# A row maximum that skips NaN: two engines in place on 16-bit halves, 64 KB loads, groups of rows with their own store

## The chip, the cores and the metric

One core of a Trainium2 chip. All times are device microseconds (us) of one execution; a kernel's time is the median of its runs. The experiments were spread over three chips; the kernel before, run beside each, took 1297.36 to 1297.54 us on all three, so I subtract their times. ACT is ScalarE, DVE is VectorE, POOL is GpSimd, SP is the queue that issues the loads.

## The reference

```python
x = np.random.randn(32, 2048, 2048).astype(np.float32)   # 537 MB
x[np.random.rand(32, 2048, 2048) < 0.1] = np.nan
return np.nanmax(x, axis=-1).astype(np.float32)           # 65536 results
```

There are 65536 rows of 2048 numbers: 512 rows for each of the 128 partitions. Every byte is read once, so the loads alone set a floor.

## The kernel before

It reads the floats as integers. ACT turns each into a key, the square of its distance from a large constant, so that NaN gets a large key and the greatest float the smallest. DVE takes the minimum. A load brings 4 rows to each partition (4 MB in all).

```python
io = ctx.enter_context(tc.tile_pool(name="io", bufs=3))      # loads, 32 KB per partition each
keys = ctx.enter_context(tc.tile_pool(name="keys", bufs=2))  # keys, another 32 KB each
for m in range(M):                                           # 128 times
    xt = io.tile([P, C, D], i32)
    nc.sync.dma_start(out=xt, in_=x_ck[m])
    kt = keys.tile([P, C, D], f32)
    nc.scalar.activation(out=kt, in_=xt, func=Square, bias=bias_t, scale=SCALE)
    nc.vector.tensor_reduce(out=acc[:, m, :], in_=kt, axis=X, op=min)
# ... cut: a square root on ACT with two Newton steps on DVE for all 512 columns,
# ... 64 transposes of 32 x 32 to bring the results into the order of the output, one store
```

The activation writes to another buffer, so a load buffer is free again as soon as ACT has read it.

Of the kernel before, what the change touches and what calls it, by code (L numbers as in the profile page):

```python
# [1 line left out]

# [4 lines left out]


@with_exitstack  # L10
def kernel(
    ctx: ExitStack,
    tc: tile.TileContext,
    x: bass.AP,
    axis: bass.AP,
    out: bass.AP,
):
    nc = tc.nc
    P = nc.NUM_PARTITIONS
    f32 = mybir.dt.float32  # L20
    i32 = mybir.dt.int32

    nd = len(x.shape)
    assert axis in (-1, nd - 1), axis
    D = x.shape[-1]

    x_bits = x.bitcast(i32).flatten_outer_dims()
    R = x_bits.shape[0]
    C = 4
    assert R % (P * C) == 0  # L30
    M = R // (P * C)
    x_ck = x_bits.rearrange("(m p c) d -> m p c d", p=P, c=C)

    out_flat = out.flatten_outer_dims().rearrange("r c -> (r c)")
    out_pn = out_flat.rearrange("(q s) -> q s", q=P)

    CG = float(0x50000000)
    SCALE = 2.0**-31
    BIAS = -CG * SCALE

    io = ctx.enter_context(tc.tile_pool(name="io", bufs=3))
    keys = ctx.enter_context(tc.tile_pool(name="keys", bufs=2))
    sing = ctx.enter_context(tc.tile_pool(name="sing", bufs=1))

    bias_t = sing.tile([P, 1], f32)
    nc.vector.memset(bias_t, BIAS)  # L46
    acc = sing.tile([P, M, C], f32)

    for m in range(M):
        xt = io.tile([P, C, D], i32)  # L50
        nc.sync.dma_start(out=xt, in_=x_ck[m])  # L51
        kt = keys.tile([P, C, D], f32)
        nc.scalar.activation(  # L53
            out=kt,
            in_=xt,
            func=mybir.ActivationFunctionType.Square,
            bias=bias_t,
            scale=SCALE,
        )
        nc.vector.tensor_reduce(  # L60
            out=acc[:, m, :],
            in_=kt,
            axis=mybir.AxisListType.X,
            op=mybir.AluOpType.min,
        )

    NQ = M * C
    accf = acc.rearrange("p m c -> p (m c)")
    y = sing.tile([P, NQ], f32)
    nc.scalar.activation(y, accf, mybir.ActivationFunctionType.Sqrt)  # L70
    for it in range(2):
        r = sing.tile([P, NQ], f32, tag=f"nr{it}")
        nc.vector.reciprocal(r, y)  # L73
        t = sing.tile([P, NQ], f32, tag=f"nt{it}")
        nc.vector.tensor_mul(t, accf, r)  # L75
        s = sing.tile([P, NQ], f32, tag=f"ns{it}")
        nc.vector.tensor_add(s, t, y)  # L77
        y = sing.tile([P, NQ], f32, tag=f"ny{it}")
        nc.vector.tensor_scalar_mul(y, s, 0.5)  # L79
    gf = sing.tile([P, NQ], f32)  # L80
    nc.scalar.activation(  # L81
        gf,
        y,
        mybir.ActivationFunctionType.Copy,
        bias=CG,
        scale=-(2.0**31),
    )
    gb = sing.tile([P, NQ], i32)
    nc.vector.tensor_copy(out=gb, in_=gf)  # L89

    B = 32
    assert M % P == 0
    U = M // P
    fin = sing.tile([P, U, P, C], i32)
    g4 = gb.rearrange("p (q u c) -> p q u c", u=U, c=C)
    for u in range(U):
        for j in range(C):
            for bi in range(P // B):
                for bj in range(P // B):
                    nc.vector.transpose(  # L100
                        out=fin[bi * B : (bi + 1) * B, u, bj * B : (bj + 1) * B, j],
                        in_=g4[bj * B : (bj + 1) * B, bi * B : (bi + 1) * B, u, j],
                    )
    nc.sync.dma_start(
        out=out_pn, in_=fin.rearrange("q u p c -> q (u p c)").bitcast(f32)
    )


# [1 line left out]
_INS = ['x', 'axis']  # L110
_OUTS = [((32, 2048), 'float32')]
#: Inputs that are plain numbers.
_NUMBERS = {'axis': -1}


# [26 lines left out]
```

## Time and profile before

1297.49 us (3 runs, 1297.33 to 1297.58). The head of the page gives each engine's busy time:

```profile
span 1295.8 us, 761 instructions
DVE 1138.4 (88%) x202; ACT 915.4 (71%) x132; POOL 0.2 (0%) x4
...
q1 hardware_dynamic: 18576, 537.14, 96.4%
```

The windows view gives the main part without start and end (columns: stretch, its length, busy us of each engine with its instructions, clock, share of DMA engines busy, GB/s):

```profile
core 0: us, DVE busy (x) ACT busy (x) POOL busy (x), PEclk, DMA share, GB/s
100.00:1200.00 1100.00, 982.71 (x114) 805.41 (x114) 0.00 (x0) 1.00 1.00 432
```

The DMA engines are never idle there: this kernel is bound by its loads, at 432 GB/s. The groups of instructions give what the stages take (after the bar: busy us, mean ns of one; after the second bar: idle us before, and what ended it):

```profile
L60 DVE TENSOR_REDUCE acc<-kt 128x4 f32<-128x8192 f32 x128 | 1111.7, 8686 | 151.2 <-ACT kt L53 151.2
L53 ACT ACTIVATE kt<-xt,bias_t 128x8192 f32<-128x8192 int32 x128 | 911.6, 7122 | 329.1 <-DMA xt<-in_x_dram 329.1
```

And the waits of the load queue say who frees the buffers (us in total, times, longest):

```profile
SPq L51 <- ACT kt L53: 899.4, 125, 8.5
SPq L51 <- DMA xt<-in_x_dram: 277.6, 125, 11.0
```

The timeline of the end (start us, us, engine, operation):

```profile
1247.91 7.12 ACT L53 ACTIVATE kt<-xt,bias_t 128x8192 f32<-128x8192 int32 x1 [2.58 <-DMA xt<-in_x_dram]
...
1255.06 8.69 DVE L60 TENSOR_REDUCE acc<-kt 128x4 f32<-128x8192 f32 x1 [1.02 <-ACT kt L53]
1263.78 0.63 ACT L70 ACTIVATE y<-acc 128x512 f32<-128x512 f32 x1 [7.45 <-DVE acc L60]
...
1276.17 16.70 DVE L100 STREAM_TRANSPOSE fin<-gb 32x32 int32<-32x32 int32 x64
1292.89 0.35 SPq L104 DMA_DIRECT2D out_dram<-fin  x1
```

The last load landed at 1247.8; the remaining 48 us are a tail in which nothing is loaded.

### The profile page before, as it was taken

Reading aid. Unit: us, or ns where it says so; the run is one execution under the profiler, and the core shown is the slowest. Engines: PE = TensorE matmul, PEld = TensorE weight load, DVE = VectorE, ACT = ScalarE, POOL = GpSimd, SP = SyncE. Lnnn points to the kernel's source line nnn. Section 1 sums busy time; section 2 is a strip of 40 time slices with the busy share of each in tenths; the row PEclk is TensorE's granted clock in tenths of the full one; section 3 lists DMA queues with packets and bytes.
Section 4 is the critical chain, followed back from the end, with each engine's and each line's share of the span. In section 5 each row is a group of like instructions: output and inputs, shape, how many; then the busy total and the mean of one; then the engine's idle time right before and its main releaser. Section 6 shows DMA issues by size and latency. Waiting matters only on the chain.

```text
span 1295.8 us, 761 instructions
## 1 busy us (share of the span) xinstructions
DVE 1138.4 (88%) x202; ACT 915.4 (71%) x132; POOL 0.2 (0%) x4
## 2 busy tenths in 40 slices
DVE  3988988988988988998998998998898998998998
ACT  4776776776776777777777777777777777777760
POOL 0000000000000000000000000000000000000000
DMA  9999999999999999999999999999999999999940
GB/s 405 437 426 432 437 429 429 437 433 426 435 432 428 434 433 427 435 435 425 435 435 425 436 434 426 435 435 426 433 436 428 431 436 430 429 436 430 429 196 8
DMA packets 18582, 537.19 MB, mean 415 GB/s; under 512 B 2064, under 2 KB 2064, under 8 KB 2192
## 3 DMA queue, kind: packets, MB, share of 16 engines
q1 hardware_dynamic: 18576, 537.14, 96.4%
q14 instruction: 6, 0.05, 0.0%
HBM read 536.87 MB, written 0.26 MB: 415 GB/s over the span
## 4 chain that ended last, share of the span: by engine, by line
DMA 73%; ACT 24%; DVE 3%; issue 0%; ACTq 0%; SPq 0%; DVEq 0%
DMA xt<-in_x_dram 73%; ACT kt L53 24%; DVE fin L100 1%; DVE acc L60 1%; DVE r L73 1%; DVE t L75 0%; DVE s L77 0%; DVE y L79 0%; ACTq L53 0%; ACT y L70 0%; ACT gf L81 0%; DVE gb L89 0%; SPq L51 0%; DVEq L137 0%
## 5 line engine op out<-in xcount | busy, mean ns | idle before, releaser
L60 DVE TENSOR_REDUCE acc<-kt 128x4 f32<-128x8192 f32 x128 | 1111.7, 8686 | 151.2 <-ACT kt L53 151.2
L53 ACT ACTIVATE kt<-xt,bias_t 128x8192 f32<-128x8192 int32 x128 | 911.6, 7122 | 329.1 <-DMA xt<-in_x_dram 329.1
L100 DVE STREAM_TRANSPOSE fin<-gb 32x32 int32<-32x32 int32 x64 | 15.8, 248 | 0.9
L53 ACT ACT_TABLE_LOAD x1 | 1.3, 1283 | 13.1 <-DMA xt<-in_x_dram 13.1
L81 ACT ACTIVATE gf<-y 128x512 f32<-128x512 f32 x1 | 0.6, 629 | 10.6 <-DVE y L79 10.6
L73 DVE RECIPROCAL r<-y 128x512 f32<-128x512 f32 x2 | 6.7, 3353 | 0.7 <-ACT y L70 0.7
L70 ACT ACTIVATE y<-acc 128x512 f32<-128x512 f32 x1 | 0.6, 629 | 7.5 <-DVE acc L60 7.5
L75 DVE TENSOR_TENSOR t<-acc,r 128x512 f32<-128x512 f32 x2 | 1.4, 693 | 0.1
L77 DVE TENSOR_TENSOR s<-t,y 128x512 f32<-128x512 f32 x2 | 1.4, 691 | 0.1
L70 ACT ACT_TABLE_LOAD x1 | 1.3, 1283 | 0.0
L89 DVE CAST gb<-gf 128x512 int32<-128x512 f32 x1 | 0.4, 427 | 0.7 <-ACT gf L81 0.7
L79 DVE TENSOR_SCALAR y<-s 128x512 f32<-128x512 f32 x2 | 0.9, 426 | 0.1
L46 DVE MEMSET bias_t<- 128x1 f32 x1 | 0.1, 59 | 0.8 <-PEq L123 0.8
L123 POOL MEMSET const-bfloat16-1.0<- 128x1 bf16 x1 | 0.1, 102 | 0.0
L123 POOL MEMSET const-uint8-127<- 128x1 uint8 x1 | 0.1, 102 | 0.0
L123 POOL MEMSET const-float32-0.0<- 128x1 f32 x1 | 0.1, 99 | 0.2 <-issue 0.2
L123 POOL MEMSET const-float32-1.0<- 128x1 f32 x1 | 0.1, 99 | 0.0
## 6 DMA issues: line engine op xcount, KB each, us to landing
xt<-in_x_dram SPq DMA_DIRECT2D x128, 4096.0 KB, 21.9
out_dram<-fin SPq DMA_DIRECT2D x1, 256.0 KB, 2.0
```

Of the source, the lines that this page charges most:

```text
L46: nc.vector.memset(bias_t, BIAS)
L53: nc.scalar.activation(out=kt, in_=xt, func=mybir.ActivationFunctionType.Square, bias=bias_t, scale=SCALE,)
L60: nc.vector.tensor_reduce(out=acc[:, m, :], in_=kt, axis=mybir.AxisListType.X, op=mybir.AluOpType.min,)
L70: nc.scalar.activation(y, accf, mybir.ActivationFunctionType.Sqrt)
L73: nc.vector.reciprocal(r, y)
L75: nc.vector.tensor_mul(t, accf, r)
L77: nc.vector.tensor_add(s, t, y)
L79: nc.vector.tensor_scalar_mul(y, s, 0.5)
L81: nc.scalar.activation(gf, y, mybir.ActivationFunctionType.Copy, bias=CG, scale=-(2.0**31),)
L89: nc.vector.tensor_copy(out=gb, in_=gf)
L100: nc.vector.transpose(out=fin[bi * B : (bi + 1) * B, u, bj * B : (bj + 1) * B, j], in_=g4[bj * B : (bj + 1) * B, bi * B : (bi + 1) * B, u, j],
L123: nc = _bacc.Bacc("TRN2", target_bir_lowering=False, num_devices=1)
```

## The change

Its intent: larger loads (8 rows, 64 KB per partition), no separate key buffers, so that three such loads fit, and almost no tail. ACT and POOL rewrite the upper 16 bits of each float in place, so that every NaN becomes a number below all others; DVE takes a plain float maximum, which is already the result. Rows are dealt out in groups in which a partition's results lie next to each other in the output, so the transposes go; each group has its own small finish (`none`, `fin`) and store; the last loads become shorter and shorter.

```diff
+GROUPS = [(40, [8] * 5)] * 12 + [(24, [7, 6, 5, 4, 2]), (8, [2, 2, 1, 1, 1, 1])]
     io = ctx.enter_context(tc.tile_pool(name="io", bufs=3))
-    keys = ctx.enter_context(tc.tile_pool(name="keys", bufs=2))
+    res = ctx.enter_context(tc.tile_pool(name="res", bufs=3))
 ... (cut)
+    for s, cuts in GROUPS:
 ... (cut: xg and og, the group's part of the input and of the output; at counts its rows)
+        acc = res.tile([P, s], f32, tag="acc")
+        for c in cuts:
+            xt = io.tile([P, c * D], i32, tag="xt")
+            nc.sync.dma_start(out=xt, in_=xg[:, at : at + c]...)
+            nc.scalar.activation(out=xt.bitcast(u16)[:, 1::2], in_=xt.bitcast(i16)[:, 1::2],
+                func=Prelu, bias=top, scale=-1.0, alpha=...)
+            nc.gpsimd.tensor_scalar(out=xt.bitcast(i16)[:, 1::2], in0=xt.bitcast(u16)[:, 1::2],
+                scalar1=-1.0, scalar2=float(TOP), op0=mult, op1=add)
+            nc.vector.tensor_reduce(out=acc[:, at : at + c], in_=xt.bitcast(f32)..., op=max)
+        none = res.tile([P, s], i32, tag="none")
+        nc.vector.tensor_scalar(out=none, in0=acc, ..., op0=is_equal, op1=mult)
+        fin = res.tile([P, s], i32, tag="fin")
+        nc.vector.tensor_tensor(out=fin, in0=acc.bitcast(i32), in1=none, op=bitwise_or)
+        nc.scalar.dma_start(out=og, in_=fin)
-    (cut: the square root, Newton steps, transposes and the one store at the end)
```

More of the change, by code (lines that the diff above doesn't have):

```diff
@@ L7 @@
 from concourse._compat import with_exitstack
+GROUPS = [(40, [8] * 5)] * 12 + [
+    (24, [7, 6, 5, 4, 2]),
+    (8, [2, 2, 1, 1, 1, 1]),
+]
+TOP = 0x7F7F
+NAN = 0x7FC0
+LOW = -129
+EDGE = TOP + 0.25
+NONE = -255.0 * 2.0**120
 @with_exitstack
@@ L19 @@
     P = nc.NUM_PARTITIONS
-    f32 = mybir.dt.float32
-    i32 = mybir.dt.int32
+    f32, i32 = mybir.dt.float32, mybir.dt.int32
+    i16, u16 = mybir.dt.int16, mybir.dt.uint16
+    ALU = mybir.AluOpType
     nd = len(x.shape)
@@ L25 @@
     D = x.shape[-1]
-    x_bits = x.bitcast(i32).flatten_outer_dims()
-    R = x_bits.shape[0]
-    C = 4
-    assert R % (P * C) == 0
-    M = R // (P * C)
-    x_ck = x_bits.rearrange("(m p c) d -> m p c d", p=P, c=C)
-    out_flat = out.flatten_outer_dims().rearrange("r c -> (r c)")
-    out_pn = out_flat.rearrange("(q s) -> q s", q=P)
-    CG = float(0x50000000)
-    SCALE = 2.0**-31
-    BIAS = -CG * SCALE
+    xr = x.bitcast(i32).flatten_outer_dims()
+    R = xr.shape[0]
+    of = out.bitcast(i32).flatten_outer_dims().rearrange("r c -> (r c)")
@@ L41 @@
+    assert R == P * sum(s for s, _ in GROUPS)
     io = ctx.enter_context(tc.tile_pool(name="io", bufs=3))
-    keys = ctx.enter_context(tc.tile_pool(name="keys", bufs=2))
+    res = ctx.enter_context(tc.tile_pool(name="res", bufs=3))
     sing = ctx.enter_context(tc.tile_pool(name="sing", bufs=1))
-    bias_t = sing.tile([P, 1], f32)
-    nc.vector.memset(bias_t, BIAS)
-    acc = sing.tile([P, M, C], f32)
-    for m in range(M):
-        xt = io.tile([P, C, D], i32)
-        nc.sync.dma_start(out=xt, in_=x_ck[m])
-        kt = keys.tile([P, C, D], f32)
-        nc.scalar.activation(
-            out=kt,
-            in_=xt,
-            func=mybir.ActivationFunctionType.Square,
-            bias=bias_t,
-            scale=SCALE,
-        )
-        nc.vector.tensor_reduce(
-            out=acc[:, m, :],
-            in_=kt,
-            axis=mybir.AxisListType.X,
-            op=mybir.AluOpType.min,
-        )
@@ L67 @@
-    NQ = M * C
-    accf = acc.rearrange("p m c -> p (m c)")
-    y = sing.tile([P, NQ], f32)
-    nc.scalar.activation(y, accf, mybir.ActivationFunctionType.Sqrt)
-    for it in range(2):
-        r = sing.tile([P, NQ], f32, tag=f"nr{it}")
-        nc.vector.reciprocal(r, y)
-        t = sing.tile([P, NQ], f32, tag=f"nt{it}")
-        nc.vector.tensor_mul(t, accf, r)
-        s = sing.tile([P, NQ], f32, tag=f"ns{it}")
-        nc.vector.tensor_add(s, t, y)
-        y = sing.tile([P, NQ], f32, tag=f"ny{it}")
-        nc.vector.tensor_scalar_mul(y, s, 0.5)
@@ L80 @@
-    gf = sing.tile([P, NQ], f32)
-    nc.scalar.activation(
-        gf,
-        y,
-        mybir.ActivationFunctionType.Copy,
-        bias=CG,
-        scale=-(2.0**31),
-    )
-    gb = sing.tile([P, NQ], i32)
-    nc.vector.tensor_copy(out=gb, in_=gf)
-    B = 32
-    assert M % P == 0
-    U = M // P
-    fin = sing.tile([P, U, P, C], i32)
-    g4 = gb.rearrange("p (q u c) -> p q u c", u=U, c=C)
-    for u in range(U):
-        for j in range(C):
-            for bi in range(P // B):
-                for bj in range(P // B):
-                    nc.vector.transpose(
-                        out=fin[bi * B : (bi + 1) * B, u, bj * B : (bj + 1) * B, j],
-                        in_=g4[bj * B : (bj + 1) * B, bi * B : (bi + 1) * B, u, j],
-                    )
@@ L104 @@
-    nc.sync.dma_start(
-        out=out_pn, in_=fin.rearrange("q u p c -> q (u p c)").bitcast(f32)
-    )
+    top = sing.tile([P, 1], f32)
+    nc.vector.memset(top, EDGE)
+    r0 = 0
+    for s, cuts in GROUPS:
+        assert sum(cuts) == s
+        xg = xr[r0 : r0 + P * s].rearrange("(p s) d -> p s d", p=P)
+        og = of[r0 : r0 + P * s].rearrange("(p s) -> p s", p=P)
+        r0 += P * s
+        acc = res.tile([P, s], f32, tag="acc")
+        at = 0
+        for c in cuts:
+            xt = io.tile([P, c * D], i32, tag="xt")
+            nc.sync.dma_start(
+                out=xt, in_=xg[:, at : at + c].rearrange("p c d -> p (c d)")
+            )
+            nc.scalar.activation(
+                out=xt.bitcast(u16)[:, 1::2],
+                in_=xt.bitcast(i16)[:, 1::2],
+                func=mybir.ActivationFunctionType.Prelu,
+                bias=top,
+                scale=-1.0,
+                alpha=float(TOP - LOW) / (EDGE - NAN),
+            )
+            nc.gpsimd.tensor_scalar(
+                out=xt.bitcast(i16)[:, 1::2],
+                in0=xt.bitcast(u16)[:, 1::2],
+                scalar1=-1.0,
+                scalar2=float(TOP),
+                op0=ALU.mult,
+                op1=ALU.add,
+            )
+            nc.vector.tensor_reduce(
+                out=acc[:, at : at + c],
+                in_=xt.bitcast(f32).rearrange("p (c d) -> p c d", c=c),
+                axis=mybir.AxisListType.X,
+                op=ALU.max,
+            )
+            at += c
+        none = res.tile([P, s], i32, tag="none")
+        nc.vector.tensor_scalar(
+            out=none,
+            in0=acc,
+            scalar1=NONE,
+            scalar2=float(0x00C00000),
+            op0=ALU.is_equal,
+            op1=ALU.mult,
+        )
+        fin = res.tile([P, s], i32, tag="fin")
+        nc.vector.tensor_tensor(
+            out=fin, in0=acc.bitcast(i32), in1=none, op=ALU.bitwise_or
+        )
+        nc.scalar.dma_start(out=og, in_=fin)
```

## The prediction

> **What bounds it now.** The load stream. By the windows view, from 100 to 1200 us the DMA engines are 100% busy at 432 GB/s, with DVE busy 983 and ACT 805 of 1100 us; one 4 MB load lands every 9.715 us (128: 1244 us). The chain of waits is 73% loads, 24% the activation that frees their buffer. That takes 7.12 us, so up to three loads are queued and their latency (the first: issued 0.7, landed 13.1 us, against 9.7 us between landings: about 2.3 us fixed) is hidden. After the last landing, at 1247.9 (timeline), come 48 us of tail: activation 7.1, reduction 8.7, square root and Newton 12, 64 transposes 16.7, store 2.
>
> **What the change takes away.** Most of that tail. With a last load of one row per partition I estimate 2 us ACT + 2 to 3 POOL + 2.2 DVE + two small operations + 2 us store: about 10 us. So up to 38 us are to be won, if loads keep streaming. Larger loads can win about 1% (432 now, 437 in the best slice).
>
> **What it adds.** A buffer is now held through all stages, as each works in place. Per 8-row load (16384 elements a partition):
> - transfer: 8.39 MB at 435 GB/s, 19.3 us, plus 2.3 us latency;
> - ACT: 14.0 us (2 x 7.12 less one fixed part): half the bytes but as many elements. The Trainium skill ("ScalarE: Activation LUTs", What ACT_TABLE_LOAD costs) gives one element per cycle for fp32 and bf16 alike; the trace agrees for 32 bits (7.12 us for 8192);
> - POOL: no such duration in the trace. The Trainium skill ("GPSIMD Engine Reference", Performance versus the Vector engine) gives 1.03 cycles per element at 1.2 GHz for at most two operations, about 1.8 for another loop: estimated 14 us, or 25 us. No run here shows it yet;
> - DVE: 2 x 8.69, 17.3 us, unchanged in total.
>
> Sum with the best POOL: 67 us. Three buffers give one load per 22.3 us, against 19.4 now for the same bytes. No engine is then the limit: the ring of three buffers is, and latency is exposed, as usually one load is in flight. A recurrence of my own with these durations (in-order engines, three buffers, all 71 loads) gives 1485 us at POOL 0.86 ns per element, 1323 at 0.4, 1607 at 1.2, 1748 at 1.58, where POOL itself is busiest. To break even POOL would have to take about 7 us per load, over two elements per nanosecond. I lean to about 0.9 ns. I assume the stores on the ACT queue, which wait for the reduction, seldom stop the next activation; if always, add 200 us.
>
> **Predicted time: 1500 us**, 8 in 10 between 1390 and 1770. Faster by over 2%: 0.06; within 2%: 0.05; slower by over 2%: 0.89.
>
> **What the profile should show.** DMA busy share down from 96% to about 83%; full loads landing every 22 to 23 us; the load queue waiting for the DVE reduction, not for ACT; POOL about 14 to 16 us per full load, 900 to 1000 in all; DVE reductions still near 1100 us in total, about 74% of the span; DVE waiting for POOL, ACT for DMA; about 10 us between the last landing and the end.
>
> **What would make it wrong.** POOL far slower (then the time is 64 times its duration per load), or far faster than one element per cycle; ACT or POOL different on 16-bit elements at a 4-byte step; POOL and DVE slowing each other; stores blocking ACT between row groups. If the time lies below 1297, the ring must have turned in under 58 us, and a stage duration above is wrong.

## The result, and the profile after

The changed kernel took 1748.09 us (4 runs, 1747.08 to 1749.83) against 1297.41 (4 runs of the kernel before): a ratio of 1.3475, 95% interval 1.3456 to 1.3494. The result was right.

```profile
span 1746.5 us, 655 instructions
DVE 1143.4 (65%) x100; ACT 1182.0 (68%) x72; POOL 1174.7 (67%) x75
...
q1 hardware_dynamic: 10224, 536.88, 72.6%
```

```profile
core 0: us, DVE busy (x) ACT busy (x) POOL busy (x), PEclk, DMA share, GB/s
100.00:1600.00 1500.00, 1004.48 (x79) 1046.28 (x57) 1026.63 (x56) 1.00 0.75 317
```

No engine is busy for more than about 70%, and the DMA engines for only 75% of the main part. Nothing is at its limit, which points to a cycle of waits rather than to an engine. The groups, kept apart by shape:

```profile
L77 ACT ACTIVATE xt<-xt,top 128x16384 uint16<-128x16384 int16 x60 | 1105.7, 18433 | 474.4 <-DMA xt<-in_x_dram 263.8 <-DVE fin L110 210.6
L85 POOL TENSOR_SCALAR xt<-xt 128x16384 int16<-128x16384 uint16 x60 | 1099.8, 18331 | 522.5 <-ACT xt L77 522.3
L93 DVE TENSOR_REDUCE acc<-xt 128x8 f32<-128x16384 f32 x60 | 1033.1, 17218 | 578.1 <-POOL xt L85 578.1
L101 DVE TENSOR_SCALAR none<-acc 128x40 int32<-128x40 f32 x12 | 38.7, 3226 | 0.4
```

The load queue now waits for the reduction, not for ACT:

```profile
SPq L74 <- DVE acc L93: 1676.5, 67, 55.4
```

A full load takes 22.0 us from issue to landing (60 of them, median):

```profile
xt<-in_x_dram SPq DMA_DIRECT2D x60, 22.0
```

A stretch of the ACT timeline, seven activations and two stores:

```profile
538.88 18.39 ACT L77 ACTIVATE xt<-xt,top 128x16384 uint16<-128x16384 int16 x1 [1.29 <-DMA xt<-in_x_dram]
575.97 0.34 ACTq L113 DMA_DIRECT2D out_dram<-fin  x1
576.41 18.43 ACT L77 ACTIVATE xt<-xt,top 128x16384 uint16<-128x16384 int16 x1 [19.15 <-DVE fin L110]
595.23 18.67 ACT L77 ACTIVATE xt<-xt,top 128x16384 uint16<-128x16384 int16 x1 [0.39 <-DMA xt<-in_x_dram]
615.03 18.42 ACT L77 ACTIVATE xt<-xt,top 128x16384 uint16<-128x16384 int16 x1 [1.14 <-DMA xt<-in_x_dram]
652.93 18.42 ACT L77 ACTIVATE xt<-xt,top 128x16384 uint16<-128x16384 int16 x1 [19.48 <-DMA xt<-in_x_dram]
672.81 18.39 ACT L77 ACTIVATE xt<-xt,top 128x16384 uint16<-128x16384 int16 x1 [1.45 <-DMA xt<-in_x_dram]
709.90 0.34 ACTq L113 DMA_DIRECT2D out_dram<-fin  x1
710.34 18.42 ACT L77 ACTIVATE xt<-xt,top 128x16384 uint16<-128x16384 int16 x1 [19.14 <-DVE fin L110]
```

Every third activation uses the same buffer. From 538.88 to 615.03 that buffer took 76.2 us for a turn. The sum of its stages is 22.0 (issue to landing) + 18.43 + 18.33 + 17.22 = 76.0, so this buffer was hardly idle; and the trace has every one of the 68 loads after the first three issued 0.03 us after the reduction that frees its buffer. So the ring of three buffers is the limit, at 76/3 = 25.3 us per load. But the next turn of that buffer, 615.03 to 710.34, took 95.3: the activation stood behind a store in the ACT queue, and the store waited for the group's result. One turn in five is lengthened in this way, and five loads take 133.8 us (519.16 to 652.93; the first of these starts lies just before the lines shown) instead of 5 x 25.3 = 127.

What of this was predicted is the ring. What was not: 18.4 instead of 14.0 us for ACT, 18.3 instead of about 14.7 for POOL, and the stores.

### The profile page after: what moved, and what is told of

Its sections match the earlier page's. It is cut to its first block, busy times and chain, and to the rows that moved or that the text cites. A ratio compares the mean times of both kernels' runs of the same rounds, so it can differ in the third digit from the quotient of the medians.

```text
span 1746.5 us, 655 instructions
## 1 busy us (share of the span) xinstructions
DVE 1143.4 (65%) x100; ACT 1182.0 (68%) x72; POOL 1174.7 (67%) x75
## 4 chain that ended last, share of the span: by engine, by line
DVE 26%; POOL 26%; ACT 22%; DMA 19%; issue 6%; ACTq 0%; POOLq 0%; DVEq 0%
POOL xt L85 26%; DVE acc L93 24%; ACT xt L77 22%; DMA xt<-in_x_dram 19%; DVE none L101 2%; ACTq L113 0%; POOLq L144 0%; DVE fin L110 0%; ACTq L77 0%; POOLq L85 0%; DVEq L93 0%
## 5 line engine op out<-in xcount | busy, mean ns | idle before, releaser
L85 POOL TENSOR_SCALAR xt<-xt 128x16384 int16<-128x16384 uint16 (+4 forms) x71 | 1174.5, 16542 | 566.4 <-ACT xt L77 565.6
L77 ACT ACTIVATE xt<-xt,top 128x16384 uint16<-128x16384 int16 (+4 forms) x71 | 1180.7, 16642 | 533.8 <-DMA xt<-in_x_dram 323.1
L93 DVE TENSOR_REDUCE acc<-xt 128x8 f32<-128x16384 f32 (+4 forms) x71 | 1102.6, 15535 | 598.9 <-POOL xt L85 598.9
L101 DVE TENSOR_SCALAR none<-acc 128x40 int32<-128x40 f32 (+2 forms) x14 | 39.1, 2790 | 0.5
```

What stands on the lines that cost most here:

```text
L77: nc.scalar.activation(out=xt.bitcast(u16)[:, 1::2], in_=xt.bitcast(i16)[:, 1::2], func=mybir.ActivationFunctionType.Prelu, bias=top, scal ...
L85: nc.gpsimd.tensor_scalar(out=xt.bitcast(i16)[:, 1::2], in0=xt.bitcast(u16)[:, 1::2], scalar1=-1.0, scalar2=float(TOP), op0=ALU.mult, op1= ...
L93: nc.vector.tensor_reduce(out=acc[:, at : at + c], in_=xt.bitcast(f32).rearrange("p (c d) -> p c d", c=c), axis=mybir.AxisListType.X, op=A ...
L101: nc.vector.tensor_scalar(out=none, in0=acc, scalar1=NONE, scalar2=float(0x00C00000), op0=ALU.is_equal, op1=ALU.mult,)
```

## The experiments

My theory: the time is that of the ring, with a stage on the 16-bit halves slower than assumed, and the stores an extra. Rivals: (a) the engines and the loads slow each other, and the stage durations are symptoms of that; (b) the stores' wait on ACT, 211 us in all, is the loss; (c) the 16-bit writes are the whole loss, whatever the buffers. The recurrence of the prediction (loads, ACT, POOL and DVE each in order; a load waits for its buffer) was run again with the durations that the trace of after shows, and with a store placed as in its ACT queue. It gives 1734 us for the changed kernel and 1662 with the stores last. It is an estimate from those durations, not a measurement.

### probe: what one stage costs by itself

Edit: all of the loop replaced by 12 activations and 11 POOL operations of 8192 elements on constant data; the stored result is wrong.

> A kernel that only measures (wrong result on purpose: it stores zeros): 12 activations and 11 POOL operations of 8192 elements each, on constant data, no loads from HBM running. Question: why were ACT (18.43 us per 16384) and POOL (18.32) both at 1.107 ns per element in the changed kernel, where the activation of before took 0.87 with its fixed part? If it is the 16-bit form itself: upper halves in place take about 9.3 us on ACT and about 9.3 us on POOL here too, and 32-bit forms 7.1 us on ACT and 7 to 8 us on POOL. If it was contention with the loads or with each other: all forms about 7.1 us here. Which of input step, output step, 16-bit input, 16-bit output makes the difference is open; I guess the 16-bit write at a 4-byte step.

Measured (one run, 221.53 us in all; the groups of instructions):

```profile
L83 ACT ACTIVATE b<-c,top 128x8192 uint16<-128x8192 int16 x1 | 9.3, 9342 | 0.0
L84 ACT ACTIVATE b<-c,top 128x8192 f32<-128x8192 int16 x1 | 7.1, 7121 | 0.0
L85 ACT ACTIVATE b<-c,top 128x8192 uint16<-128x8192 int32 x1 | 9.3, 9342 | 0.0
L87 ACT ACTIVATE b<-c,top 128x8192 uint16<-128x8192 int16 x1 | 7.1, 7121 | 0.0
...
L92 POOL TENSOR_SCALAR b<-c 128x8192 f32<-128x8192 f32 x1 | 7.0, 7017 | 81.7 <-ACT b L90 81.7
L95 POOL TENSOR_SCALAR b<-c 128x8192 int16<-128x8192 uint16 x1 | 9.2, 9237 | 0.1
L99 POOL TENSOR_SCALAR b<-c 128x8192 int16<-128x8192 uint16 x1 | 7.0, 7018 | 0.1
L100 POOL TENSOR_SCALAR b<-c 128x8192 int16<-128x8192 uint16 x1 | 22.9, 22927 | 0.1
```

The lines don't show the element step, so here it is: L83 reads and writes upper halves (16 bits every 4 bytes); L84 reads halves and writes contiguous 32-bit words; L85 reads words and writes halves; L87 reads halves and writes 16-bit elements without gaps; L92 is words to words; L95 halves to halves; L99 halves to gapless 16-bit. All forms but L100, on both engines (a gapless read with halves written was run on ACT only):

| 8192 elements | ACT us | POOL us |
|---|---|---|
| 32-bit to 32-bit, in place or not | 7.12 | 7.02 |
| halves read, 32-bit written | 7.12 | 7.02 |
| 16-bit written without gaps | 7.12 | 7.02 |
| halves written, read from words, halves or gapless | 9.34 to 9.40 | 9.24 to 9.26 |

Among these forms the 16-bit write at a 4-byte step is the one thing that costs, and it costs the same here without any load as in the changed kernel (the 4-row load at its end: ACT 9.36, POOL 9.26). Most of these operations also ran while the other two engines did nothing. Rival (a) falls as far as the durations go. bf16 halves took 9.34 and 9.24, as the integer halves did. L100 is the exception, and no part of the argument: the same halves with one operation instead of two took 22.93 us on POOL, and why stays open.

### stores_last: only the ACT queue's order changed

```diff
-        nc.scalar.dma_start(out=og, in_=fin)
+        stores.append((og, fin))
+    with tc.issue_after(act.ins):        # behind the last activation
+        for og, fin in stores:
+            nc.scalar.dma_start(out=og, in_=fin)
```

(The result tiles get 14 buffers, so that all stay alive.)

> The changed kernel with nothing but the order of the ACT queue altered: all 14 stores stand behind the last activation. Ring theory (three buffers, each held for load 22.0 + ACT 18.4 + POOL 18.3 + DVE 17.2 = 76 us, so one load per 25.3 us; stores are an extra on top): 1660 to 1680 us. Store theory (the 211 us for which ACT waited for the group results are the loss beyond the ring, all on the critical path): about 1535 us. No effect: 1748.

Measured 1671.73 us (ratio to before 1.2884), result right. The stores cost 1748 - 1672 = 76 us, not 211: most of ACT's wait for them would have been a wait for the next load anyway. Rival (b) falls as the main cause; it stands as one of three terms. The 76 us are a net figure: the small `none` operations of DVE, 39 us in all in the changed kernel, now take 88 us, for a reason given further below (POOL and DVE).

```profile
L102 DVE TENSOR_SCALAR none<-acc 128x40 int32<-128x40 f32 (+2 forms) x14 | 87.7, 6266 | 0.5
```

### rows4 and rows4_last: the same bytes in twice as many buffers

```diff
-GROUPS = [(40, [8] * 5)] * 12 + [(24, [7, 6, 5, 4, 2]), (8, [2, 2, 1, 1, 1, 1])]
+GROUPS = [(40, [4] * 10)] * 12 + [(24, [4] * 6), (8, [2, 2, 1, 1, 1, 1])]
-    io = ctx.enter_context(tc.tile_pool(name="io", bufs=3))
+    io = ctx.enter_context(tc.tile_pool(name="io", bufs=6))
```

rows4 has nothing else; rows4_last also has the edit of stores_last.

> The changed kernel with loads of 4 rows and six buffers: the same 192 KB per partition, the same bytes, elements, engines and store order. Ring theory: a buffer is held for 12 + 9.4 + 9.3 + 8.7 = 39 us, over six buffers 6.6 us per 4 MB load, less than the 9.7 us of the transfer, so the loads are the limit again but for the stores: my recurrence gives 1360 us. Contention theory (the engines slow each other or the loads, whatever the split): stays at 1650 to 1750.

> Loads of 4 rows, six buffers, and the stores behind the last activation. Ring theory: no limit but the loads, recurrence 1266 us, so 2% under the kernel before, DMA engines busy over 97%. If the stores did nothing: as rows4. Contention theory: above 1600.

Measured: rows4 1358.33 us (1.0467 of before), rows4_last 1280.76 us (0.987, interval 0.9856 to 0.9885: clear of 1, but within 2% of it), both right. The elements, the bytes, the engines and the memory used are those of the changed kernel; only the cut differs, and rows4 is 390 us faster. So contention between the engines or with the loads, rival (a), isn't the main loss. In rows4_last the loads run as before the change:

```profile
100.00:1200.00 1100.00, 995.19 (x138) 1057.89 (x114) 1046.70 (x114) 1.00 1.00 432
```

The recurrence is 15 us too low for rows4_last. It assumes 435 GB/s; at the 432 measured, 537 MB take 9 us more. And from its timeline, the first loads of the short end land while ACT is still working: ACT runs six activations without a gap from 1228.96 to 1254.89, and the last load is taken up only at 1261.05, since it had to wait for its buffer until a reduction ended at 1256.39.

### word32_last: the stages that the prediction had assumed

The 8-row kernel with the stores last, but both stages in place on 32-bit words (wrong result):

```diff
-            nc.scalar.activation(out=xt.bitcast(u16)[:, 1::2], in_=xt.bitcast(i16)[:, 1::2], func=Prelu, ...)
-            nc.gpsimd.tensor_scalar(out=xt.bitcast(i16)[:, 1::2], in0=xt.bitcast(u16)[:, 1::2], ...)
+            nc.scalar.activation(out=xt.bitcast(f32), in_=xt, func=Square, bias=top, scale=2.0**-31)
+            nc.gpsimd.tensor_scalar(out=xt.bitcast(f32), in0=xt.bitcast(f32), ...)
```

> The 8-row kernel with the stores last, and both in-place stages on 32-bit elements instead of the upper halves (the Square of before on ACT, a 32-bit multiply-add on POOL; wrong result on purpose). The probe says 14.0 us for ACT and 13.9 for POOL per load, where the 16-bit writes take 18.4 and 18.3. Ring theory: (22.0 + 14.0 + 13.9 + 17.2)/3 = 22.4 us per load at most, recurrence 1468 us, against 1672 with the 16-bit stages; this is the case that the prediction had assumed. If the 16-bit writes alone were the loss and the ring none: back at about 1300. If stage durations off the busiest engine did not matter: 1670.

Measured 1477.36 us (1.1385 of before). ACT took 13.95 and POOL 13.85 us per load:

```profile
L78 ACT ACTIVATE xt<-xt,top 128x16384 f32<-128x16384 int32 x60 | 836.9, 13948 | 496.2 <-DMA xt<-in_x_dram 475.3 <-DVE none L101 14.0 <-DVE acc L93 7.0
L85 POOL TENSOR_SCALAR xt<-xt 128x16384 f32<-128x16384 f32 x60 | 830.8, 13847 | 539.7 <-ACT xt L78 539.7
```

The function on ACT changed too (Square for Prelu), but in the probe both take 7.12 us on 8192 words. Rival (c) falls: with the 16-bit writes gone, 180 us of loss against the kernel before remain, and these are the ring's: every load is still issued 0.03 us after the reduction that frees its buffer. The 16-bit writes cost 1671.7 - 1477.4 = 194 us; (4.48 + 4.48)/3 us per load times 64 loads' worth of rows is 191.

### nopool_last: one stage fewer

The 8-row kernel with the stores last and the `nc.gpsimd.tensor_scalar` deleted (wrong result).

> The 8-row kernel with the stores last and the POOL stage left out (wrong result on purpose). Ring theory: (22.0 + 18.4 + 17.2)/3 = 19.2 us per load, just under the 19.3 of the transfer, so the loads are the limit again: recurrence 1275 us. If a stage that was busy for only two thirds of the time cost nothing: still about 1670.

Measured 1314.70 us (1.0135 of before). Taking out an engine that was busy for 70% of the time in stores_last saved 357 us: it was on the ring, not off the critical path. It did not reach the 1275 of the recurrence. In the windows view its main part runs at 422 GB/s, where the recurrence assumes 435, and a full load takes 24.1 us from issue to landing instead of 22.0:

```profile
100.00:1200.00 1100.00, 955.77 (x78) 1017.23 (x57) 0.00 (x0) 1.00 0.99 422
xt<-in_x_dram SPq DMA_DIRECT2D x60, 24.1
```

For the 60 full loads the rate makes 36 of the 40 us (503 MB at 422 and at 435 GB/s: 1193 and 1157 us). The expected turn of (22.0 + 18.4 + 17.2)/3 = 19.2 us per load left out that two loads are then in flight for part of the time (1.2 on average from 100 to 1200 us, by the trace, against 0.84 in the changed kernel). With 24.1 the sum is 59.7 and the step 19.9 us, which is what the trace shows from one full load to the next. So the ring is still the limit here, if only just. That the overlap is what lengthens the landing is argued, not shown.

### rows2_last and rows2_mid: still smaller loads

```diff
-GROUPS = ...
+GROUPS = [(40, [2] * 20)] * 12 + [(24, [2] * 12), (8, [2, 2, 1, 1, 1, 1])]
-    io = ctx.enter_context(tc.tile_pool(name="io", bufs=3))
+    io = ctx.enter_context(tc.tile_pool(name="io", bufs=12))
```

rows2_last has the stores last; rows2_mid issues eleven of them 14 loads after their group.

> Loads of 2 rows, twelve buffers, stores last, right result. Ring theory: (7 + 4.8 + 4.7 + 4.4)/12 = 1.7 us per 2 MB load, far below its 4.83 us of transfer, so loads are the limit, but ACT at 4.82 us per load is just as slow as they are. The end is shorter by half a stage. Recurrence 1253 us; as the recurrence was 14 us short for 4 rows, I expect 1255 to 1270. If loads of 16 KB per partition ran slower than those of 32 and 64 KB: above 1280.

> As rows2_last, but the store of each of the first eleven groups stands in the ACT queue 14 loads after its group's end, where its result is long done, so 3 stores instead of 14 stand at the end. If the row of stores at the end costs time: 3 to 8 us below rows2_last; if not: equal, and the early stores block nothing.

Measured 1277.67 and 1278.00 us (0.9848 and 0.985 of before: like rows4_last, within 2%), right. Both lie above the 1255 to 1270 expected. In the window the loads run at 428 GB/s, and ACT is busy for 98%:

```profile
100.00:1200.00 1100.00, 996.12 (x249) 1080.76 (x225) 1059.35 (x225) 1.00 1.01 428
```

It is tempting to call ACT the new limit: an activation takes 4.83 us for 2 rows, as long as the transfer. But the trace of rows2_last says that it only just keeps up. The chain that ended last is made of loads, and the load queue waits for earlier loads, hardly for a buffer:

```profile
DMA xt<-in_x_dram 98%; POOL xt L86 1%; DVE acc L94 1%; SPq L75 0%; DVE none L102 0%; DVE fin L111 0%; POOLq L86 0%; DVEq L94 0%
SPq L75 <- DMA xt<-in_x_dram: 1127.2, 250, 5.5
```

Each load is issued 0.06 us (median) after the one eight places before it has landed, and the activation starts 0.08 us after its load's landing all through the main part, just as in rows4_last; in rows4, where ACT with its stores does set the pace, it starts about 16 us after the landing (median). (ACT's idle moments, 0.07 us each, are too short for the waits view to list.) So the loads are the limit here too, at one per 4.89 us, or 428 GB/s instead of the 432 of 4 MB loads. Over 537 MB that is 11 us; no run tests whether the size of the loads is the reason, and the rest of the miss wasn't taken apart. Where the stores stand makes no difference here: the row of stores at the end costs nothing that can be seen.

### keys_groups: the tail's half of the change alone

The two stages and the buffers of before, with the change's row groups, a finish and store per group, and short last loads; the square root starts from an integer guess, so that ACT is not needed for it:

```diff
-    x_ck = x_bits.rearrange("(m p c) d -> m p c d", p=P, c=C)
+    GROUPS = [(40, [4] * 10)] * 12 + [(24, [4] * 6), (8, [2, 2, 1, 1, 1, 1])]
 ... loads, Square into keys (bufs=2) and min as before, per group ...
-    nc.scalar.activation(y, accf, mybir.ActivationFunctionType.Sqrt)
-    for it in range(2):
+        nc.vector.tensor_scalar(out=y, in0=acc.bitcast(i32), scalar1=0.5, scalar2=float(0x1FBD1DF5), op0=mult, op1=add)
+        for it in range(3):
-    (64 transposes, one store)
+        (gpsimd or, for the last group, sync).dma_start(out=og, in_=fin)
```

> The other half of the change alone: the two stages and buffers of the kernel before (4-row loads, 3 load buffers, Square on ACT into 2 buffers of 32-bit keys, minimum on DVE; no POOL, nothing in place), with the change's row groups, a finish and a store per group, and tapered last loads. The square root starts from an integer guess and takes three Newton steps on DVE (the finish of before used ACT); the 64 transposes go, as each partition's results of a group are contiguous in the output. The load stream should be as before (9.715 us per 4 MB, last landing near 1248 us); the tail should be 2.0 ACT + 2.3 DVE + about 14 small DVE operations of 0.2 us + a 2 us store = 9 to 13 us in place of 48. Expected 1255 to 1265 us, 3% under the kernel before. If the loads slow down with the row-group layout or the finish holds up the reductions: 1280 or more.

Measured 1271.59 us, right; ratio 0.9801, interval 0.9785 to 0.9818: the fastest of all, and surely faster than before; whether by 2% is unclear, as the interval lies on both sides of 0.98. The load stream is untouched (432 GB/s from 100 to 1200 us). The gain is smaller than I expected. By the timeline, in the short loads at the end ACT waits for DVE to empty one of the two key buffers, so load buffers come free late, and the last load lands at 1257.0 instead of near 1248 (no run tests this reading):

```profile
1237.41 13.01 DVE L66 TENSOR_REDUCE acc<-kt 128x4 f32<-128x8192 f32 x2 [1.03 <-ACT kt L59]
1246.13 3.71 ACT L59 ACTIVATE kt<-xt,bias_t 128x4096 f32<-128x4096 int32 x1 [5.16 <-DVE acc L66]
...
1259.50 2.00 ACT L59 ACTIVATE kt<-xt,bias_t 128x2048 f32<-128x2048 int32 x1 [0.28 <-DVE acc L66]
```

### All together

| kernel | us | recurrence |
|---|---|---|
| before | 1297.4 | |
| changed | 1748.1 | 1734 |
| changed, stores last | 1671.7 | 1662 |
| the same, 32-bit stages (wrong result) | 1477.4 | 1468 |
| the same as stores last, no POOL (wrong result) | 1314.7 | 1275 |
| 4 rows, 6 buffers | 1358.3 | 1360 |
| 4 rows, 6 buffers, stores last | 1280.8 | 1266 |
| 2 rows, 12 buffers, stores last | 1277.7 | 1253 |
| stages of before, groups and short last loads | 1271.6 | |

## Why the prediction was right or wrong

The prediction was 1500 us, with a range of 1390 to 1770 that holds the 1748 measured, and 0.89 for slower. But it forecast a loss of 203 us where 451 came. The mechanism was right; two terms of its sum were too small. That the prediction's recurrence has the very figure 1748 in its list is chance: it stands there for a POOL of 1.58 ns per element that is itself the limit, while POOL took 1.12 (18.33 us for 16384) and was busy for 67%.

- **The ring: right.** "Three buffers give one load per 22.3 us ... No engine is then the limit: the ring of three buffers is." With about the stage durations assumed, and no store in the way (word32_last), the chip took 1477 us; the recurrence for the prediction had said 1485. Half the bytes per buffer with twice the buffers, or one stage fewer, takes most of the loss away. The load queue waits for the reduction, as foretold. (The fixed latency of a load, given as 2.3 us, is 13.1 - 0.7 - 9.7 = 2.7 by the prediction's own figures, and 22.0 - 19.3 = 2.7 in the trace of after: small.)
- **The step that failed: "ACT: 14.0 us (2 x 7.12 less one fixed part): half the bytes but as many elements"**, and with it "I lean to about 0.9 ns" for POOL. Both measured 1.11 ns per further element, 18.4 and 18.3 us per load (from the operations on 16384 and on 2048 elements: (18433 - 2544)/14336 on ACT, (18331 - 2458)/14336 on POOL). Worth 194 us. The activation of before showed only a 32-bit write, and the Trainium skill ("ScalarE: Activation LUTs", What ACT_TABLE_LOAD costs) gives one rate for fp32 and bf16. That holds in the probe for 16-bit integers written without gaps, 7.12 us; it does not hold for 16-bit writes every 4 bytes, integer or bf16, 9.34 us. The same is true of POOL: the 1.03 cycles per element of the Trainium skill ("GPSIMD Engine Reference", Performance versus the Vector engine) are what the probe shows for 8192 elements to 32-bit words (7.02 us at the page's 1.2 GHz is 1.03 cycles), but halves take 9.24.
- **The second term: "I assume the stores on the ACT queue ... seldom stop the next activation; if always, add 200 us."** They stopped it 11 times, at nearly every group, because the store stands one activation after its group's last while the result needs POOL and DVE as well. Cost: 76 us, not 200, as a delayed activation finds its load ready and some of the lost time would have been waiting.
- The parts: 1477 (ring) + 194 (16-bit writes) + 76 (stores) = 1748. As each part is the difference of two neighbouring runs, this sum closes by construction; what bears it out is that the 194 agree with the 191 from the durations alone, and the recurrence with 1748 within 1%. Against the 1500 predicted this means 270 us too little for the two terms, and 23 too much elsewhere.
- **"POOL and DVE slowing each other": small, and in one place.** The reductions took 17.22 us, as expected from those of before. But the tiny `none` operation took 3.2 us on average instead of 0.18. Two of them in the timeline:

```profile
157.80 18.32 POOL L85 TENSOR_SCALAR xt<-xt 128x16384 int16<-128x16384 uint16 x1 [1.04 <-ACT xt L77]
...
174.04 2.12 DVE L101 TENSOR_SCALAR none<-acc 128x40 int32<-128x40 f32 x1
...
1711.91 0.18 DVE L101 TENSOR_SCALAR none<-acc 128x24 int32<-128x24 f32 x1
```

  The first ends at 176.16, just after POOL's operation ends at 176.12; the longest lasts 12.73 us, and ends at 1652.81, where POOL's ends at 1652.77. The one at 1711.91 meets an idle POOL. The Trainium skill ("SBUF — State Buffer", Who interferes with whom) says that DVE's tensor_scalar can take a port pair that it shares with GpSimd, that the later one is fully blocked until the first is done, and that tensor_reduce never contends. The trace can't show a port, but it agrees with the rest: all 12 `none` operations that start beside a POOL operation end 0.04 us after it, and the reductions keep their time. A run settles that POOL is the cause: in nopool_last, without it, none of the 14 took more than 0.185 us. The 39 us of these operations (88 in stores_last) are part of the times above; no run took them out alone.
- **The tail: right.** "About 10 us between the last landing and the end": the last load was issued at 1731.2 and its kind lands in 4.7 us, and the span ends at 1746.5. But no run that keeps the loads going won all of the 38 us: the best, keys_groups, won 26.
- **The shape of the profile: as predicted, but scaled.** DMA busy 73% rather than 83%, a full load per 26.8 us with stores rather than 22 to 23, POOL 1175 us in all rather than 900 to 1000.

## What to carry to other kernels

Working in place makes a buffer's turn the sum of load latency, transfer and every stage; divide that by the number of buffers before asking which engine is busiest, and where it exceeds the transfer time cut the tiles smaller and take more of them: here the same memory cut in six instead of three was worth 390 us. Three buffers can never keep all four stages (load, ACT, POOL, DVE) at work; in the main part of the changed kernel their busy shares, 0.75 + 0.70 + 0.68 + 0.67, come to 2.8. In such a ring every stage costs, also on engines that are busy for two thirds of the time, so a duration assumed for it should be measured in its exact form, with the step of its writes. A store that waits for a later engine must not stand in the queue of an earlier one close behind the work that it waits for.

## What the Trainium skill lacked or had wrong

- ScalarE: Activation LUTs (What ACT_TABLE_LOAD costs): one element per cycle for fp32 and bf16 alike is stated without a word on the step of the writes. For 16-bit elements it held here only where they were written without gaps: a 16-bit write at a 4-byte step took 9.34 us for 8192 elements against 7.12, and 1.11 ns per further element; the step of the reads made no difference.
- GPSIMD Engine Reference (Performance pitfalls for Q7 kernels): it names a cost for reads at a wide step, none for writes. 16-bit writes at a 4-byte step took 9.24 us against 7.02 for 8192 elements, reads at that step nothing extra.
- The same page (Performance versus the Vector engine): a POOL tensor_scalar with a single add, halves to halves, took 22.93 us where multiply and add together took 9.24. No page has this; one instruction in one run shows it, its cause was not looked for, and no single-operation form with other data was tried.
- SBUF — State Buffer (Who interferes with whom): right here, but its one figure for a slowed DVE, 6.8 times, gives no idea of the harm to a small operation: one on 40 columns that takes 0.18 us took up to 12.73 us beside a POOL operation (71 times as long), and up to 16.31 us in stores_last.
